# A three-layer transformer forward pass on one core: SBUF addresses of the moving operands shifted against those of the weights

## Chip, core and metric

The program runs on one core of a Trainium2 chip. The metric is device time in microseconds (us), median of the runs shown. TensorE (PE) does the matrix products, VectorE (DVE) and ScalarE (ACT) the elementwise work, GpSimd (POOL) a little of it, and SyncE's queue (SP) issues nearly all loads. "Product" below means one matmul instruction, which multiplies a 128x128 stationary operand (the weights, loaded by an instruction of its own, PEld) with a moving operand of 128 partitions and 128 to 512 columns.

## What is computed

One block with modulation from a vector `c` (pooling, forgetting attention and a gated recurrence side by side, then a gated feed-forward with a causal convolution), a norm, and then two layers of a second kind (three sorts of attention, then a feed-forward with squared ReLU). 256 tokens, 2048 features, float32 throughout. Cut to the products, which hold the work:

```python
mod = silu(c) @ w_ada + b_ada
h = rmsnorm(x, g_mix) * (1 + sc1) + sh1
x = x + gt1 * (mixer(h @ w_in) @ w_out)
h = rmsnorm(x, g_ffn) * (1 + sc2) + sh2
x = x + gt2 * ((silu(conv(h @ w_gate)) * (h @ w_up)) @ w_down)   # 5632 hidden
x = rmsnorm(x, final_g)
for l in range(2):
    x = x + attention(rmsnorm(x) @ w_in_2[l]) @ w_o_2[l]
    x = x + relu(rmsnorm(x) @ w_up_2[l]) ** 2 @ w_down_2[l]       # 8192 hidden
out = rmsnorm(x, norm_final_2)
```

## The kernel before

Activations lie with the features on the partitions: `x`, and its two parts `xh` and `xl` (high and low, both float32r, together called X below), are tiles of 16 row tiles x 256 tokens, 1024 bytes to a row tile and partition. A float32 product is done as three float32r products: high weights by high activations (line 332), high by low (333), low by high (334); `mm_b` on these lines makes nearly all of the work. The weights come from DRAM in pieces of 512 KB (`Unit`): SP loads one to a `raw` tile (seven buffers), ACT rounds it to `whi` (line 136), DVE subtracts to `wlo` (line 137; three buffers each), and PE uses them in 24 products with the 256 tokens as moving operand. In a few places `mm_a` (lines 347 to 349) has it the other way round: slices of `xh` and `xl` are the weights, and `whi` or `wlo`, 256 or 512 columns, is the moving operand.

The order is written out by hand: a list of units is walked in order, splits run up to three units ahead, and small jobs (softmax, norms, convolutions) are generators that advance one stage after each unit. Nothing reorders the instructions afterwards.

The moving operands of `mm_b` are these tiles: X for the projections into a block; `xn` for the pooled and the recurrent part in `w_out`; `uh` and `ul` for `w_ffn_down`; `u0` and `u1` (named `u` in the profile) for `w_down_2`; `mb` for a quarter of `w_o_2`; each with `whi` or `wlo` as the weights.

Tiles are laid in SBUF in the order in which the pools ask for them. The pool `cp`, open for the whole program, has `params`, `ident`, some small tiles, then (lines 490 to 502) `mod` (96 floats to a partition), `cact` (16), `gsc`, `fgg`, `x`, `xh`, `xl` and the rest. The pool `st` behind it holds `raw`, `whi` and `wlo`. On top of both lies the pool of the phase, opened and closed as the program goes: `ffnp` for the first feed-forward has `uh` and `ul` at its foot (line 1138), `mlp0` and `mlp1` for the others have `u0` and `u1` there (line 1801). In the built program each row of `whi` and `wlo` that a product uses as weights starts at a byte address of 192 modulo 512 in its partition. The rows of the moving operands start at: X 160, `uh`, `ul`, `u0` and `u1` 192, `xn` 480, `mb` 0. A row tile being 1024 bytes, every row of a tile has the same residue. As distances from the weights, modulo 512: X 480, `uh`/`ul`/`u` 0, `xn` 288, `mb` 320. In `mm_a`, where `whi` and `wlo` (192) move over X (160), the distance is 32.

Of the kernel before, what the change touches and what calls it, by code (L numbers as in the profile page):

```python
# [17 lines left out]
P = 128  # L18
# [39 lines left out]
def shape_constants():  # L58
    """Arrays that follow from the shapes alone."""
    half = np.arange(P) // 64  # L60
    block = (half[:, None] == half[None, :]).astype(np.float32)
    q = np.arange(S)
    causal = np.where(q[None, :] <= q[:, None], 0.0, NEG).astype(np.float32)
    causal = causal.reshape(2, P, S).transpose(1, 0, 2).reshape(P, 2 * S)
    c = np.arange(64)
    cs = np.clip(c - 8, 0, 48)
    near = np.where((c[None, :] >= cs[:, None]) & (c[None, :] < cs[:, None] + 16), 0.0, NEG)
    near = np.tile(near, (2, 1)).astype(np.float32)
    freqs = np.float32(10000.0) ** (-np.arange(0, 32, 2, dtype=np.float32) / np.float32(32))
    p = np.arange(P) % 64  # L70
    pos = np.where((p // 32 == 0)[:, None], (q // 64)[None, :], (q % 64)[None, :]).astype(np.float32)
    ang = (pos * freqs[p % 16][:, None]).astype(np.float32).astype(np.float64)
    cos = np.cos(ang).astype(np.float32)
    sin = (np.sin(ang) * np.where(p % 32 < 16, -1.0, 1.0)[:, None]).astype(np.float32)
    rec = np.stack([1.0 / np.minimum(np.arange(1, 17), w) for w in WINDOWS]).astype(np.float32)
    rec = np.broadcast_to(rec.reshape(1, 64), (P, 64))
    tri = (np.arange(P)[:, None] <= np.arange(P)[None, :]).astype(np.float32)
    rel = np.arange(-255, 256)
    n = np.abs(rel)
    nf = np.maximum(n, 1).astype(np.float32)  # L80
    large = 8 + (np.log(nf / np.float32(8)) / np.float32(np.log(16.0)) * np.float32(8)).astype(np.int32)
    bucket = np.where(rel > 0, 16, 0) + np.where(n < 8, n, np.minimum(large, 15))
    bucket = np.where(n > 128, 32, bucket)
    onehot = np.zeros((33, 511), np.float32)
    onehot[bucket, np.arange(511)] = 1.0
    return {
        "ident": np.eye(P, dtype=np.float32),
        "mixc": np.ascontiguousarray(np.concatenate([causal, rec, tri], axis=1)),
        "blkc": np.ascontiguousarray(np.concatenate([block, cos, sin, near], axis=1)),
        "onehot": onehot,  # L90
    }
# [27 lines left out]
class Unit:  # L119
    """A [128, nk, ncols] piece of a weight: loaded, cut into two float32r parts, used on the tensor engine."""  # L120
# [24 lines left out]
class Ada:  # L145
    """128 rows x 1024 columns of w_ada times silu(c), summed over the row tiles on the vector engine."""
# [44 lines left out]
def weave(a, b):  # L191
    """the two lists, evenly interleaved"""
# [7 lines left out]
class Builder:  # L200
# [41 lines left out]
    def take(self, tag, shape, dt=F32):  # L242
        """waits (in stages) for a free buffer of the phase pool; returns (number, tile)"""
        while not self.slots[tag]:
            yield
        i = self.slots[tag].popleft()
        return i, self.ph.tile(shape, dt, tag=f"{tag}{i}", name=tag)
# [4 lines left out]
    def bank(self):  # L252
        """the same for a PSUM bank"""
# [23 lines left out]
    def more_groups(self):  # L277
        """two of the banks go over to the column groups"""
# [3 lines left out]
    def fewer_groups(self):  # L282
        """the column groups leave them again; put back once what is in them has been read"""
# [37 lines left out]
    def mm_b(self, u, ps, X, first, last, k0=None, ncols=None):  # L321
        """PSUM[nb] += W[:, nb].T X for the rows of one unit; X = (hi, lo), features on the partitions."""
# [13 lines left out]
    def mm_a(self, u, outs, X, first, last, c0, n, shared=False):  # L336
        """outs[half] += X[:, half].T W for the rows of one unit: tokens on the partitions."""
# [13 lines left out]
    def split_to(self, hi, lo, src, scale=1.0):  # L351
        """hi + lo = src * scale, both float32r."""
# [13 lines left out]
    def units(self, w, kts, c0, ncols, use):  # L366
        """kts: (first row tile, number of row tiles) of each unit"""
        return [Unit(self, w, k, n, c0, ncols, use, i) for i, (k, n) in enumerate(kts)]

    def group(self, w, c0, ncols, kts, X, evac, k0=None, state=None, part="all"):  # L370
        """Units of one column group whose sum stays in PSUM; evac(banks) is a generator started at its end."""
# [17 lines left out]
    def sumsq_add(self, acc, src, first, scale=1.0):  # L389
        """acc (+)= (src * scale)^2"""  # L390
# [8 lines left out]
    def tok_sums(self, ps, *tiles):  # L399
        """Sum over the partitions of tiles of [128, n x 256] -> PSUM [128 tokens, 2]."""  # L400
# [9 lines left out]
    def rstd_of(self, r, ss, n):  # L410
        """r = (ss / n + eps) ** -0.5 of [128, 2]"""
# [9 lines left out]
    def bcast(self, ps, r, dg):  # L421
        """r [128 tokens, 2] -> PSUM [128, 256], each token's value in all partitions."""
# [4 lines left out]
    def rms_now(self, squares, out):  # L427
        """out [128, 256] = 1 / rms of x by token, from tiles of squares"""
# [6 lines left out]
    def rms(self, acc, flag):  # L435
        """the same in stages, to rtok and rbc"""
# [40 lines left out]
    def run(self):  # L477
        tc, nc, io = self.tc, self.nc, self.io
        with ExitStack() as es:
# [10 lines left out]
            self.mod = cp.tile([P, 96], F32, name="mod")  # L490
            self.cact = cp.tile([P, 16], F32, name="cact")
# [4 lines left out]
            self.xl = cp.tile([P, KT, S], F32R, name="xl")  # L496
            self.X = (self.xh, self.xl)
# [31 lines left out]
    def ada_end(self, acc, srcs, then, wait):  # L529
        """the sums over the partitions, to mod; then what needs them"""  # L530
# [20 lines left out]
    def prep(self, q, src, g, sh0, sc0, flag, need=None):  # L551
        """X = src * g * (1 + scale) + shift for four row tiles"""
# [17 lines left out]
    def need(self, flag):  # L570
        """X, once the row tiles of the unit are prepared"""
# [7 lines left out]
    # ================= block 1: mixer =================  # L579
# [6 lines left out]
    def log1p_exp(self, out, e, w):  # L586
        """out = log(1 + e) for 0 <= e <= 1, by the odd series in e / (2 + e); w: three tiles to work in"""
# [15 lines left out]
    def mixer(self):  # L603
# [27 lines left out]
        # silu(c)  # L631
# [7 lines left out]
        # x with features on the partitions, and x / rms(x)  # L639
# [8 lines left out]
        def turn(k):  # L648
            """two row tiles of x and of x / rms(x), the latter by products with a diagonal matrix"""
# [20 lines left out]
        def consts():  # L670
# [5 lines left out]
            # cl = -4 softplus(-lambda), 4 softplus(-lambda)  # L676
# [11 lines left out]
            # halves of the gate biases  # L688
# [16 lines left out]
        # the last two groups of a quarter of the rows stay in PSUM and are the first of the next one  # L705
# [3 lines left out]
        def add_z(name, q, pv, keep):  # L709
            """z (+)= the two banks"""  # L710
# [42 lines left out]
        def forget():  # L753
            """F = cumsum(log sigmoid(f + b)): fq with the tokens on the partitions, fs by head in the first rows of a tile"""
# [100 lines left out]
        # w_out: rows of the recurrent and the pooled part first, the attention rows after  # L855
# [52 lines left out]
    def recurrent(self):  # L908
# [21 lines left out]
        # gelu(y): 0.5 y (1 + tanh(sqrt(2/pi) (y + 0.044715 y^3))), the 0.5 with the product below  # L930
# [19 lines left out]
        # ti = (1 + ti) * xc  (twice the gated input)  # L950
# [13 lines left out]
        # -expm1(2 log_a) = th (1 + a^2), th = tanh(-log_a); its root as v * v^-0.5  # L964
# [19 lines left out]
        # 0.5 of the gate and 0.5 of the gelu  # L984
# [57 lines left out]
    def softmax(self, b, sc, pr, bias, sink, free=None):  # L1042
        """pr = softmax(sc + bias), by rows, with the logit sink beside; frees the bank b"""
# [33 lines left out]
    def fox(self, h):  # L1077
        """One head of the forgetting attention; logits + F[q] - F[k] under the causal mask"""
# [46 lines left out]
    # ================= block 1: gated feed-forward =================  # L1125
# [3 lines left out]
    def ffn(self):  # L1129
# [4 lines left out]
        def start():  # L1134
            self.open_pool("ffnp")
            self.slots["sg"] = deque(range(2))
            ph = self.ph
            F["uh"] = ph.tile([P, KT, S], F32R, name="uh")
# [11 lines left out]
        def gate(j0, g):  # L1150
            """sg = silu(conv(g)) of hidden row tiles j0 .. j0 + 3"""
# [18 lines left out]
        def up(j0, slot, ps):  # L1170
            """rows slot .. slot + 3 of the hidden layer: gate times the two banks in ps"""
# [37 lines left out]
        def acc_units(g, q):  # L1209
            """rows of quarter q for column group g (even: gate, odd: up) of the first 2048 hidden columns"""  # L1210
# [18 lines left out]
        def pair(j0, slot0):  # L1229
            """gate and up of four hidden row tiles"""  # L1230
# [54 lines left out]
        def end():  # L1285
            # x2 = x r1 final_g; its own rstd r2 goes to the next products together with r1
# [47 lines left out]
    def lead(self):  # L1334
        """puts the loads of w_ada, one for one, before the weights of the first block, LEAD ahead"""
# [11 lines left out]
    # ================= block 2 =================  # L1347
    def bias_tables(self):
        """The position biases, spread to [head, query, key] in DRAM."""
# [51 lines left out]
    def layer(self, l):  # L1401
# [4 lines left out]
        def start():  # L1406
# [18 lines left out]
            # row tiles 0-3: A, 4-7: B, 8-15: C; queries, then the heads' outputs  # L1425
# [20 lines left out]
        def kk(dst, c, raw):  # L1446
            """dst[:, 0, c] / [:, 1, c]: high / low part of one head's keys, in both halves of the partitions"""
# [4 lines left out]
        def queries(qs, raw):  # L1452
            """two heads' queries: [high; low] and [low; high]"""
# [5 lines left out]
        def rope(t, gain, done):  # L1459
            """norm per head and rotary embedding of two row tiles, in place"""  # L1460
# [98 lines left out]
        def head(h, keys, v, table, sink, near, kpair, need, values, last):  # L1559
            """one head; queries and output in row tile h // 2"""  # L1560
# [75 lines left out]
        def norm(name, t0, n, dst, d0, gain, after):  # L1636
            """the heads' outputs, normalised over all heads of the kind"""
# [30 lines left out]
        def v_units(name, c0, n, kts, done):  # L1668
            """the values of n heads, tokens on the partitions"""
# [53 lines left out]
        def mb():  # L1723
            # in the place of the outputs of A and the first half of C, which are in X by then
# [73 lines left out]
        def mid():  # L1798
            self.close_pool()
            self.open_pool(f"mlp{l}")  # L1800
            L["u"] = [self.ph.tile([P, KT, S], F32R, name=f"u{i}") for i in range(2)]
# [134 lines left out]
```

## Time and profile before

| | us |
|---|---|
| median of 3 runs | 3420.06 (3419.43 to 3421.57) |
| span of the profiled execution, first to last instruction | 3419.7 |
| PE busy in it | 3282.7 (96%) |
| DVE busy | 2213.9 (65%) |
| ACT busy | 1629.8 (48%) |
| POOL busy | 294.4 (9%) |
| DMA | 684 MB, mean 200 GB/s |

The profiled execution ended within 0.4 us of the median, so its span can be used for it. A matmul's record is some 283 ns long, but several are under way at a time, so the time between the starts of two products that follow each other, and not the record's length, tells what one costs PE. That time is got from a stretch in which PE doesn't pause: the records that touch the stretch, divided into its length plus one record. In a view of one tile alone, it is the busy time less one record, divided by the count less one.

### The profile page before, as it was taken

Reading aid. Unit: us, or ns where it says so; the run is one execution under the profiler, and the core shown is the slowest. Engines: PE = TensorE matmul, PEld = TensorE weight load, DVE = VectorE, ACT = ScalarE, POOL = GpSimd, SP = SyncE. Lnnn points to the kernel's source line nnn. Section 1 sums busy time; section 2 is a strip of 40 time slices with the busy share of each in tenths; the row PEclk is TensorE's granted clock in tenths of the full one; section 3 lists DMA queues with packets and bytes.
Section 4 is the critical chain, followed back from the end, with each engine's and each line's share of the span. In section 5 each row is a group of like instructions: output and inputs, shape, how many; then the busy total and the mean of one; then the engine's idle time right before and its main releaser. Section 6 shows DMA issues by size and latency. Waiting matters only on the chain.

```text
span 3419.7 us, 64015 instructions
## 1 busy us (share of the span) xinstructions
PE 3282.7 (96%) x26612; PEld 3231.9 (95%) x26612; DVE 2213.9 (65%) x2921; ACT 1629.8 (48%) x2236; POOL 294.4 (9%) x250
## 2 busy tenths in 40 slices
PE   7989899979999998999999999999999999999998
PEld 7988889979999998989999999998889999999998
DVE  7898887537745668976545454556897655545454
ACT  4436345424434456865434343445775533334344
POOL 0021100000000032111000000012110100000000
PEclk9999999999999999999999999999999999999999
DMA  9986896659866554545666665665454656666563
GB/s 360 336 286 224 300 318 225 187 169 304 273 200 187 184 160 122 162 143 180 185 185 185 185 186 183 186 182 154 133 161 153 182 184 185 185 185 185 183 186 125
DMA packets 390722, 683.96 MB, mean 200 GB/s; under 512 B 40823, under 2 KB 97952, under 8 KB 390176
## 3 DMA queue, kind: packets, MB, share of 16 engines
q1 hardware_dynamic: 390144, 679.56, 62.8%
q8 instruction: 208, 3.41, 0.4%
q14 instruction: 82, 0.67, 0.1%
q10 hardware_dynamic: 288, 0.31, 0.0%
HBM read 677.62 MB, written 8.46 MB: 201 GB/s over the span
## 4 chain that ended last, share of the span: by engine, by line
PE 77%; DVE 6%; DMA 2%; issue 2%; ACT 2%; SPq 1%; POOL 0%; ACTq 0%; DVEq 0%; POOLq 0%
PE pg L334 24%; PE pg L332 24%; PE pg L333 24%; DVE wlo L137 2%; ACT whi L136 1%; DMA raw<-in_w_ffn_up 1%; DMA raw<-in_w_ffn_gate 1%; DMA raw<-in_w_out 1%; PE pa L1620 1%; PE pa L1073 1%; DVE qs L1457 1%; DVE kB L362 0%; PE pa L1556 0%; DVE pr L1049 0%; DVE ada L171 0%
## 5 line engine op out<-in xcount | busy, mean ns | idle before, releaser
L137 DVE TENSOR_TENSOR wlo<-raw,whi 128x1024 fp32r<-128x1024 f32 x1064 | 1319.0, 1241 | 1089.0 <-ACT whi L136 1084.9
L136 ACT ACTIVATE whi<-raw 128x1024 fp32r<-128x1024 f32 x1064 | 1123.4, 1058 | 1554.0 <-PE pg L333 1254.1
L332 PE MATMUL pg<-xh,whi 128*128 128x256 f32 x5184 | 1478.6, 285 | 24.6 <-ACT whi L136 20.0
L334 PE MATMUL pg<-xh,wlo 128*128 128x256 f32 x5184 | 1468.2, 283 | 16.3 <-DVE wlo L137 16.2
L333 PE MATMUL pg<-xl,whi 128*128 128x256 f32 x5184 | 1467.0, 283 | 1.8 <-DVE xl L565 1.1
L332 PEld LDWEIGHTS pg<-xh,whi 128*128 128x128 f32 x5184 | 988.3, 191 | 30.4 <-ACT whi L136 21.2
L334 PEld LDWEIGHTS pg<-xh,wlo 128*128 128x128 f32 x5184 | 987.0, 190 | 20.8 <-DVE wlo L137 20.4
L333 PEld LDWEIGHTS pg<-xl,whi 128*128 128x128 f32 x5184 | 987.7, 191 | 6.9 <-issue 2.7
L332 PE MATMUL pg<-u,whi 128*128 128x256 f32 x2048 | 579.9, 283 | 0.0
L333 PE MATMUL pg<-u,whi 128*128 128x256 f32 x2048 | 579.5, 283 | 0.0
L334 PE MATMUL pg<-u,wlo 128*128 128x256 f32 x2048 | 579.5, 283 | 0.0
L333 PEld LDWEIGHTS pg<-u,whi 128*128 128x128 f32 x2048 | 393.1, 192 | 0.0
L334 PEld LDWEIGHTS pg<-u,wlo 128*128 128x128 f32 x2048 | 393.1, 192 | 0.0
L332 PEld LDWEIGHTS pg<-u,whi 128*128 128x128 f32 x2048 | 393.1, 192 | 0.0
L171 DVE SCALAR_TENSOR_TENSOR ada<-raw,cact,ada 128x1024 f32<-128x1024 f32 x180 | 234.8, 1304 | 19.1 <-DMA raw<-in_w_ada 18.1
L397 POOL TENSOR_TENSOR acc<-acc,t 128x512 f32<-128x512 f32 (+1 forms) x73 | 97.1, 1345 | 1372.3 <-ACT t L396 1361.0
L334 PE MATMUL pg<-uh,wlo 128*128 128x256 f32 x704 | 199.3, 283 | 0.0
L332 PE MATMUL pg<-uh,whi 128*128 128x256 f32 x704 | 199.3, 283 | 0.0
L333 PE MATMUL pg<-ul,whi 128*128 128x256 f32 x704 | 199.2, 283 | 0.0
L1820 POOL TENSOR_TENSOR y<-y 128x1024 f32<-128x1024 f32 x32 | 61.6, 1927 | 1200.0 <-ACT u L1819 1200.0
L332 PEld LDWEIGHTS pg<-uh,whi 128*128 128x128 f32 x704 | 135.1, 192 | 0.9 <-issue 0.9
L334 PEld LDWEIGHTS pg<-uh,wlo 128*128 128x128 f32 x704 | 135.1, 192 | 0.2 <-DVE wlo L137 0.2
(323 smaller groups left out, 2815.8 us busy)
## 6 DMA issues: line engine op xcount, KB each, us to landing
raw<-in_w_up SPq DMA_DIRECT2D x256, 512.0 KB
raw<-in_w_down SPq DMA_DIRECT2D x256, 512.0 KB
raw<-in_w_ada SPq DMA_DIRECT2D x192, 512.0 KB
raw<-in_w_in SPq DMA_DIRECT2D x192, 512.0 KB
raw<-in_w_ffn_gate SPq DMA_DIRECT2D x88, 512.0 KB
raw<-in_w_ffn_up SPq DMA_DIRECT2D x88, 512.0 KB
raw<-in_w_ffn_down SPq DMA_DIRECT2D x88, 512.0 KB
raw<-in_w_o SPq DMA_DIRECT2D x64, 512.0 KB
```

Of the source, the lines that this page charges most:

```text
L136: b.nc.scalar.activation(hi[:, :n], self.raw[:, :n], AF.Copy)
L137: b.nc.vector.tensor_tensor(lo[:, :n], self.raw[:, :n], hi[:, :n].bitcast(F32), ALU.subtract)
L171: b.nc.vector.scalar_tensor_tensor(g["acc"], self.raw, cs, g["acc"], ALU.mult, ALU.add)
L332: mm(o, wh, xh[:, k0 + j, :], start=st, stop=False, skip_group_check=True)
L333: mm(o, wh, xl[:, k0 + j, :], start=False, stop=False, skip_group_check=True)
L334: mm(o, wl, xh[:, k0 + j, :], start=False, stop=last and j == u.nk - 1, skip_group_check=True)
L397: nc.gpsimd.tensor_tensor(acc, acc, t, ALU.add)
L1073: self.nc.tensor.transpose(ps[:, k * S + i * P : k * S + (i + 1) * P], pr[:, i, k * P : (k + 1) * P], self.ident)
L1457: nc.vector.tensor_tensor(qs[b, h, :], raw[a], qs[a, h, :].bitcast(F32), ALU.subtract)
L1620: nc.tensor.matmul(o, v()[:, k].rearrange("p a d -> p (a d)"), pt[1][:, c, k, :], start=n == 0, stop=n == 3)
L1820: nc.gpsimd.tensor_tensor(flat(y), flat(y), flat(y), ALU.mult)
```

## The change

Three places change where tiles lie; the docstrings and comments that it also takes out have no effect.

- `mod` and `cact` (384 and 64 bytes to a partition) are allocated behind `xl` instead of ahead of `gsc`. `gsc`, `fgg`, `x`, `xh` and `xl` lie 448 bytes lower; everything behind them stays where it was.
- The pool `ffnp` gets an unused tile of 160 bytes at its foot, so that `uh`, `ul` and what lies above them move up by 160.
- The pools `mlp0` and `mlp1` get one of 288 bytes, so that `u0`, `u1` and what lies above them move up by 288.

```diff
-            self.mod = cp.tile([P, 96], F32, name="mod")
-            self.cact = cp.tile([P, 16], F32, name="cact")
             self.gsc = cp.tile([P, 16], F32, name="gsc")
             self.fgg = cp.tile([P, 16], F32, name="fgg")
             self.x = cp.tile([P, KT, S], F32, name="x")
             self.xh = cp.tile([P, KT, S], F32R, name="xh")
             self.xl = cp.tile([P, KT, S], F32R, name="xl")
+            self.mod = cp.tile([P, 96], F32, name="mod")
+            self.cact = cp.tile([P, 16], F32, name="cact")
...
             self.open_pool("ffnp")
             self.slots["sg"] = deque(range(2))
             ph = self.ph
+
+            ph.tile([P, 40], F32, name="skew")
             F["uh"] = ph.tile([P, KT, S], F32R, name="uh")
             F["ul"] = ph.tile([P, KT, S], F32R, name="ul")
...
             self.open_pool(f"mlp{l}")
+            self.ph.tile([P, 72], F32, name="skew")
             L["u"] = [self.ph.tile([P, KT, S], F32R, name=f"u{i}") for i in range(2)]
```

The distances from the weights, modulo 512, are then: X 32, `uh` and `ul` 160, `u0` and `u1` 288; `xn` and `mb` stay at 288 and 320, and in `mm_a` the distance becomes 480. On every engine the built program has the same instructions in the same order with the same waits as before; only addresses differ.

## Rows read from the trace of the kernel before

**Rows 1.** The page: busy time of PE; shares of the chain that ended last.

```profile
PE 3282.7 (96%) x26612; PEld 3231.9 (95%) x26612; DVE 2213.9 (65%) x2921; ACT 1629.8 (48%) x2236; POOL 294.4 (9%) x250
...
PE 77%; DVE 6%; DMA 2%; issue 2%; ACT 2%; SPq 1%; POOL 0%; ACTq 0%; DVEq 0%; POOLq 0%
```

**Rows 2.** Groups of PE's instructions by line and shape: count, busy, mean ns, idle before.

```profile
L332 PE MATMUL pg<-xh,whi 128*128 128x256 f32 x5184 | 1478.6, 285 | 24.6 <-ACT whi L136 20.0 <-ACT xh L562 3.0 <-DVE zp L719 0.9
...
L332 PE MATMUL pg<-u,whi 128*128 128x256 f32 x2048 | 579.9, 283 | 0.0
...
L332 PE MATMUL pg<-uh,whi 128*128 128x256 f32 x704 | 199.3, 283 | 0.0
...
L347 PE MATMUL pg<-whi,xh 128*128 128x512 f32 x128 | 54.3, 424 | 7.3 <-DVE zq L721 7.1 <-ACT whi L136 0.3
...
L347 PE MATMUL pg<-whi,xh 128*128 128x256 f32 x64 | 19.5, 304 | 0.0
```

**Rows 3.** Busy time in stretches (us; engine busy, xinstructions; PEclk): tile `u` alone.

```profile
1676.00:1770.00 94.00, 92.31 (x768) 92.22 (x768) 1.37 (x2) 1.04 (x1) 1.00 0.60 184
```

**Rows 4.** The same for tile `uh` alone (two of each three products).

```profile
928.00:1021.00 93.00, 92.31 (x512) 79.92 (x512) 1.37 (x2) 1.04 (x1) 1.00 0.66 197
```

**Rows 5.** The same, all instructions, in a stretch of X alone.

```profile
1022.00:1152.00 130.00, 130.00 (x1101) 130.00 (x1100) 71.06 (x78) 58.91 (x63) 0.00 (x0) 1.00 0.60 188
```

**Rows 6.** The same for tile `xn` alone.

```profile
346.00:366.50 20.50, 19.99 (x170) 19.91 (x170) 0.00 (x0) 0.00 (x0) 0.00 (x0) 1.00 0.92 311
```

**Rows 7.** The same for tile `mb` alone.

```profile
1562.00:1586.00 24.00, 22.78 (x192) 22.68 (x192) 0.00 (x0) 0.00 (x0) 1.00 0.59 178
```

**Rows 8.** Timeline of PE (start us, us): first and last of 71 products of `mm_a`.

```profile
2359.70 0.28 PE L348 MATMUL pg<-wlo,xh 128*128 128x256 f32 x1
...
2367.87 0.28 PE L349 MATMUL pg<-whi,xl 128*128 128x256 f32 x1
```

**Rows 9.** Line 758, weights of 8 columns: shortest, median, longest ns; first, last start.

```profile
L758 PE MATMUL pa<-xh,wfh x16: 276/276/281, 207.1 to 212.2; 128*8 128x256 f32 x16
```

**Rows 10.** All engines by stage: us, PE, PEld, DVE, ACT, POOL, PEclk, DMA share, GB/s.

```profile
0.00:540.00 540.00, 484.99 (x3625) 462.23 (x3626) 456.51 (x570) 254.38 (x364) 63.31 (x83) 0.96 0.88 305
540.00:720.00 180.00, 179.17 (x1493) 177.73 (x1492) 110.03 (x129) 87.56 (x98) 0.00 (x0) 1.00 0.58 180
720.00:780.00 60.00, 41.47 (x295) 39.78 (x293) 24.43 (x26) 15.63 (x17) 0.00 (x0) 0.83 0.57 190
780.00:1232.00 452.00, 451.78 (x3796) 451.38 (x3797) 280.53 (x307) 205.71 (x233) 16.81 (x22) 1.00 0.71 224
1232.00:1512.00 280.00, 251.88 (x1890) 239.80 (x1889) 237.49 (x521) 194.85 (x410) 54.96 (x44) 0.96 0.47 142
1512.00:2340.00 828.00, 828.00 (x6953) 827.73 (x6952) 449.40 (x454) 345.00 (x362) 56.82 (x34) 1.00 0.60 183
2584.00:3400.00 816.00, 816.00 (x6855) 815.73 (x6854) 438.78 (x446) 345.73 (x372) 53.50 (x32) 1.00 0.59 179
```

**Rows 11.** The same stages, tile `xl` alone: PE, PEld, DVE, PEclk, DMA share, GB/s.

```profile
0.00:540.00 540.00, 275.38 (x935) 179.25 (x935) 16.53 (x40) 0.96 0.88 305
540.00:720.00 180.00, 67.46 (x241) 45.24 (x241) 0.00 (x0) 1.00 0.58 180
...
780.00:1232.00 452.00, 226.44 (x806) 151.97 (x807) 5.22 (x12) 1.00 0.71 224
1232.00:1512.00 280.00, 144.37 (x491) 95.52 (x491) 5.14 (x9) 0.96 0.47 142
1512.00:2340.00 828.00, 341.29 (x1216) 228.96 (x1215) 16.08 (x33) 1.00 0.60 183
2340.00:2584.00 244.00, 123.55 (x419) 81.55 (x419) 2.72 (x4) 0.96 0.47 142
2584.00:3420.00 836.00, 334.06 (x1189) 223.97 (x1189) 10.11 (x18) 0.99 0.58 177
```

## The prediction, made before the changed kernel ran

> **What bounds the kernel now.** I read the page first, for which engine fills the span: PE is busy 96% of it and makes 77% of the chain that ended last [rows 1]. Then the view by line: three lines of `mm_b` hold nearly all of PE's work, 5184 triples of products with X, 2048 with `u`, 704 with `uh` [rows 2], that is 15,552, 6144 and 2112 products. Then the stages: from 540 to 720 us, 780 to 1232, 1512 to 2340 and 2584 to 3400 PE hardly pauses (179.2 of 180 us, 451.8 of 452, 828 of 828, 816 of 816), at the full granted clock (1.00), with DVE at 54 to 62% busy and the DMA engines at 58 to 71% [rows 10]. In the first 540 us, between 720 and 780, and in the two attention stages PE pauses and others come last; there DMA (0.88 and 305 GB/s in the first 540 us) or DVE (237 of 280 us in the first attention) is close to full [rows 10].
>
> So in some 2280 us of 3420 the time is the count of products by the interval from the start of one to the next. That interval is what the change can move, and the trace has it for five distances between moving operand and weights. All are 256 columns on 128x128 weights at a granted clock of 1.00:
> - distance 0, `u`: (92.31 - 0.28) / 767 = 120.0 ns [rows 3]; `uh`/`ul`: 768 products in the same busy time (the 512 shown are the `uh` ones), again 120.0 ns [rows 4].
> - distance 480, X: (130 + 0.28) / 1101 = 118.3 ns [rows 5].
> - distance 320, `mb`: (22.78 - 0.28) / 191 = 117.8 ns [rows 7].
> - distance 288, `xn`: (19.99 - 0.28) / 169 = 116.6 ns [rows 6].
> - distance 32, `mm_a`: 8.17 us / 70 = 116.7 ns [rows 8].
>
> `u`, `uh`, `xn`, `mb` and X stand on the same three lines, with the same shape, type and clock; what differs is the tile, that is its address. A product on the same X tiles but with weights of 8 columns takes (212.2 - 207.1) / 45 = 113.3 ns [rows 9], so about 3 to 7 ns of each interval come with the load of the 128 weight columns that runs beside it. I read this as two streams of PE out of SBUF, moving operand and next weights, that get in each other's way by their relative address, most at distance 0. The moving operand's own address can't be it: `u` and the `whi` of `mm_a` both start at 192 modulo 512, and take 120.0 and 116.7 ns.
>
> [...]
>
> **The change part by part.** No instruction, order or wait is altered, so each part is a count of products by a difference of intervals.
>
> `u`, 0 to 288: after the change its rows stand at 480 modulo 512 and the weights at 192, just as those of `xn` do now. 6144 products, all in stages where PE never pauses: 6144 x (120.0 - 116.7) = 20.3 us. I take 116.7 for `xn` and `mm_a` alike; the 0.1 between them is the views' rounding.
>
> X, 480 to 32: 32 is shown by `mm_a`, with the roles of the tiles exchanged, and 288, which differs from 32 by 256, gives the same 116.7 in `mm_b`. So 118.3 to 116.7, which is 1.63 ns before rounding. One product in three with X reads `xl`, so the counts of `xl` by stage tell where X is used: 241 + 806 + 1216 + 1189 = 3452 from 540 to 720, 780 to 1232, 1512 to 2340 and after 2584 [rows 11], 10,356 products, in stages bound by PE: 16.9 us. The other stages: in the first 540 us 935, less 64 of `mm_a`, is 2613 products, 4.3 us; but DMA fills most of it, and a faster PE waits for the next load, so I count a quarter, 1.1 us. In the two attention stages 491 + 419, less 128 of `mm_a`, is 2346 products, 3.8 us; DVE is busy 85% of the first and PE 90%, and I count half, 1.9 us. The 99 or so triples between 720 and 780, where PE is busy 41.5 of 60 us [rows 10], count nothing.
>
> `uh`/`ul`, 0 to 160: no row has 160. Bounds: not above distance 0, 120.0 (no gain); not below the product with small weights, 113.3 (14.2 us). If distances that differ by 256 act alike, as 32 and 288 do, 160 lies between 64 (that is 320, 117.8) and 224 (that is 480, 118.3), and further from 0 than either. I take 117.5, halfway from the best interval with full weights, 116.7, to the interval of X: 2112 x 2.5 = 5.3 us.
>
> `mm_a`, 32 to 480: here the change goes the wrong way. 192 products of 256 columns and 384 of 512 [rows 2]. At X's present interval the first lose 1.63 ns each, 0.3 us; the others, having two 256s of columns, at most 3.3 ns, 1.3 us. They lie in the first 540 us and in the attention stages, so half: 0.8 us lost.
>
> Everything else keeps its distance: `xn`, `mb`, the attention's own products. Elementwise work gets other addresses too, but DVE and ACT have free time in the stages that PE bounds.
>
> Who would be late next in these stages? A unit of 24 products takes 2.88 us at 120.0 and 2.80 at 116.7, and wants 512 KB, which is 187 GB/s at the faster pace, against 183 now; between 780 and 1232 the loads run at 224 on average with PE full [rows 10]. DVE goes from 54% to 56%. Neither comes near.
>
> Sum: 20.3 + 16.9 + 1.1 + 1.9 + 5.3 - 0.8 = 44.7 us. From the span 3419.7 that is 3375.0; from the median 3420.06 it is 3375.4 us.
>
> **Rivals.**
> - X gains nothing: 32 is good with the roles as in `mm_a` but not with `whi` as the weights, and X stays at 118.3. Then 19.9 us fall away: 3395.3. For it: no row has distance 32 in `mm_b`. Against it: 288 in `mm_b`, and equal intervals at 32 and 288.
> - The freed time comes back as waits for DVE or loads in the PE-bound stages. If half of it did, 3397.7. Against it: the idle shares above; and between 1512 and 2340 us and between 2584 and 3400 PE waits for nobody at all.
> [...]
> - Slower: at 32 the moving rows follow so close behind the weights that they collide more than at 480. Place: X in the PE-bound stages; price, at 123 ns (as far above `u` as `u` is above 117): 10,356 x 4.7 = 48.7 us lost against 20.3 + 5.3 gained, some 3443. It decides from 118.3 + 25.6 / 10.356 = 120.8 ns on, more than any of the five distances shows.
>
> **How the numbers follow.** Forecast 0.82, X without gain 0.08, half eaten by waits 0.04, no effect 0.03, slower 0.03. The range of the forecast: if all of X's gain in the mixed stages counts (5.1 more), `uh` comes to 113.3 (9 more, unlikely at the same time) and `mm_a` costs nothing (0.8), the time is 3360.5; if the mixed stages give nothing (3.0), `uh` stays at 120.0 (5.3) and `mm_a` costs all (0.8), 3384.5. A few pauses more or less in the mixed stages, where the granted clock is 0.83 to 0.96 [rows 10] and so falls to its lower level now and then, can move it by some us on either side. I give 3362 to 3388; it leaves out all four rivals, 0.18. A measurement of this kernel can tell 0.2%, 6.8 us, from no change: faster by more than that are the forecast and the first two rivals, 0.94; within it 0.03; slower 0.03.
>
> **What would show it.** In the changed kernel's stretches: `u` at 116.7 ns a product, X at 116.7, `uh` between 116.7 and 118.3, `xn` and `mb` as now at 116.6 and 117.8, `mm_a` at 118.3; PE still full from 1512 us (or where that stage then begins) to the next attention; shorter stages after 780 us by about 1.4% for X and 2.8% for `u`. What would make it wrong: an interval for X above 118, which the exchange of roles could hide from me; new waits of PE for `whi` or `wlo` in the stages that have none; or the first 540 us changing by more than 2 us.

## The result, and the profile after

The changed kernel takes 3382.68 us (median of 4 runs, 3375.75 to 3386.76) against 3420.18 before (4 runs by now): 37.5 us less, a ratio of 0.989 (95% interval 0.9875 to 0.9903). Forecast were 3375.4 us and 44.7 us less, with a range of 3362 to 3388. The profiled execution has a span of 3381.7 us, 38.0 less than the one of before; a second set of four runs of the same kernel gave 3381.69 (3379.57 to 3383.47).

The page after: busy time by engine, and the chain that ended last.

```profile
PE 3238.2 (96%) x26612; PEld 3186.4 (94%) x26612; DVE 2213.5 (65%) x2921; ACT 1630.8 (48%) x2236; POOL 294.7 (9%) x250
...
PE 75%; DVE 7%; issue 2%; ACT 2%; DMA 2%; POOL 0%; SPq 0%; ACTq 0%; DVEq 0%; POOLq 0%
```

PE is busy 44.5 us less with the same number of instructions, DVE and ACT as long as in [rows 1]. The same products are started closer together. PE's idle time grew from 137.0 to 143.5 us: of the 44.5 us 6.5 came back as pauses. In the two long stages that PE bounds it stays full:

```profile
1508.00:2319.00 811.00, 811.00 (x6946) 810.71 (x6945) 448.95 (x454) 344.64 (x361) 56.85 (x34) 1.00 0.64 187
2581.00:3361.00 780.00, 779.94 (x6685) 779.48 (x6685) 420.96 (x417) 333.62 (x350) 53.75 (x32) 1.00 0.62 183
```

Busy time of stretches by tile shows it (us; PE, PEld and so on, each busy time with its count; granted clock, DMA share, GB/s): first `u`, which answers to [rows 3], then `uh` as in [rows 4].

```profile
1670.00:1762.00 92.00, 89.76 (x768) 89.67 (x768) 1.37 (x2) 1.05 (x1) 1.00 0.62 189
```

```profile
924.00:1018.00 94.00, 91.30 (x512) 78.76 (x512) 1.37 (x2) 1.05 (x1) 1.00 0.69 199
```

`u` went from 120.0 to (89.76 - 0.28) / 767 = 116.7 ns, `uh` here to (91.30 - 0.28) / 767 = 118.7. All instructions in stretches of one tile alone: X as in [rows 5], X in three other places, and last `uh` in another place.

```profile
1017.00:1147.00 130.00, 130.00 (x1116) 130.00 (x1116) 72.17 (x80) 60.02 (x64) 0.00 (x0) 1.00 0.65 190
831.00:920.00 89.00, 89.00 (x758) 89.00 (x757) 66.76 (x70) 40.44 (x43) 0.00 (x0) 1.00 0.90 287
564.70:620.00 55.30, 55.30 (x471) 55.30 (x471) 42.80 (x57) 30.70 (x37) 0.00 (x0) 1.00 0.63 191
1762.00:1842.00 80.00, 80.00 (x688) 80.00 (x687) 42.78 (x41) 32.70 (x32) 5.75 (x3) 1.00 0.65 190
640.00:714.00 74.00, 74.00 (x633) 74.00 (x632) 33.09 (x28) 31.18 (x34) 0.00 (x0) 1.00 0.60 183
```

X stands at 130.28 / 1116 = 116.7 ns in the first, at 89.28 / 758 = 117.8 in the second, at 55.58 / 471 = 118.0 in the third (117.8 from start to start), at 80.28 / 688 = 116.7 in the fourth; `uh` at 74.28 / 633 = 117.3. One count more or less is 0.1 to 0.3 ns here. So X has two intervals at one and the same distance, and so has `uh`. The same two views for `mb`, whose distance the change leaves at 320, in the first layer and in the second:

```profile
1556.00:1581.00 25.00, 22.78 (x192) 22.69 (x192) 0.00 (x0) 0.00 (x0) 1.00 0.63 187
```

```profile
2624.00:2649.00 25.00, 21.93 (x192) 21.84 (x192) 0.00 (x0) 0.00 (x0) 1.00 0.64 188
```

The first is as in [rows 7], 117.8 ns; the second is 113.4, at the same distance, with the same instructions and clock. And `mm_a`, whose distance went from 32 to 480, first and last of 71 products on PE's timeline (start us, duration us), as in [rows 8]:

```profile
2339.11 0.28 PE L348 MATMUL pg<-wlo,xh 128*128 128x256 f32 x1
...
2347.40 0.28 PE L349 MATMUL pg<-whi,xl 128*128 128x256 f32 x1
```

8.29 us / 70 = 118.4 ns, where it was 116.7. That is X's old interval at X's old distance, with the roles exchanged. The products of `mm_a` with 512 columns went through the same exchange; first and last of 48 in a row, before and after:

```profile
69.66 0.39 PE L347 MATMUL pg<-whi,xh 128*128 128x512 f32 x1
...
80.61 0.39 PE L349 MATMUL pg<-whi,xl 128*128 128x512 f32 x1
```

```profile
69.35 0.40 PE L347 MATMUL pg<-whi,xh 128*128 128x512 f32 x1
...
80.31 0.40 PE L349 MATMUL pg<-whi,xl 128*128 128x512 f32 x1
```

10.95 / 47 = 233.0 ns at 32 and 10.96 / 47 = 233.2 at 480, at a granted clock of 1.00: the products of 512 columns show no effect of this distance.

### The profile page after: what moved, and what is told of

The parts are those of the page before. It is cut to its first block, busy times and chain, and to the rows that moved or that the text cites. A ratio compares the mean times of both kernels' runs of the same rounds, so it can differ in the third digit from the quotient of the medians.

```text
span 3381.7 us, 64015 instructions
## 1 busy us (share of the span) xinstructions
PE 3238.2 (96%) x26612; PEld 3186.4 (94%) x26612; DVE 2213.5 (65%) x2921; ACT 1630.8 (48%) x2236; POOL 294.7 (9%) x250
## 4 chain that ended last, share of the span: by engine, by line
PE 75%; DVE 7%; issue 2%; ACT 2%; DMA 2%; POOL 0%; SPq 0%; ACTq 0%; DVEq 0%; POOLq 0%
PE pg L334 24%; PE pg L332 24%; PE pg L333 24%; DVE wlo L137 3%; ACT whi L136 1%; DMA raw<-in_w_ffn_up 1%; DMA raw<-in_w_ada 1%; DVE ada L171 1%; DVE qs L1459 1%; PE pa L1622 1%; PE pa L1073 1%; DVE kB L362 0%; PE pa L1558 0%; DVE pr L1049 0%; DVE y L1489 0%
## 5 line engine op out<-in xcount | busy, mean ns | idle before, releaser
L332 PE MATMUL pg<-u,whi 128*128 128x256 f32 x2048 | 572.1, 279 | 0.0
L333 PE MATMUL pg<-u,whi 128*128 128x256 f32 x2048 | 571.7, 279 | 0.0
L334 PE MATMUL pg<-u,wlo 128*128 128x256 f32 x2048 | 571.6, 279 | 0.0
L333 PEld LDWEIGHTS pg<-u,whi 128*128 128x128 f32 x2048 | 384.9, 188 | 0.0
L334 PEld LDWEIGHTS pg<-u,wlo 128*128 128x128 f32 x2048 | 384.9, 188 | 0.0
L332 PEld LDWEIGHTS pg<-u,whi 128*128 128x128 f32 x2048 | 384.9, 188 | 0.0
```

The lines of the kernel that those rows point to most:

```text
L332: mm(o, wh, xh[:, k0 + j, :], start=st, stop=False, skip_group_check=True)
L333: mm(o, wh, xl[:, k0 + j, :], start=False, stop=False, skip_group_check=True)
L334: mm(o, wl, xh[:, k0 + j, :], start=False, stop=last and j == u.nk - 1, skip_group_check=True)
```

## The experiments

All are edits of the kernel before, and the profiles are of one execution each. "Interval" is the time from the start of one product of 256 columns to the next, in a stretch in which PE doesn't pause; "distance" is always moving operand from weights, modulo 512.

**One edit at a time.** `x_only` has the first edit alone, `u_only` the third.

> The first of the three edits alone: X moves from distance 480 to 32, u and uh stay at 0. Theory A (the distance between moving operand and weights sets the interval): X at 116.7 ns in most stretches, at 117.8 in some, as in the changed kernel; u and uh at 120.0. Stretches of X shorter by 1.28 us per 768 products; in all 12 to 16 us less than before, about 3405. Theory B (the interval belongs to the tile or to its own address, not to the distance): X could go anywhere; u and uh as before too.

> The third edit alone: u moves from distance 0 to 288, X stays at 480, uh at 0. Theory A: u at 116.7 ns, 2.54 us less per 768 products, 20.3 us in all, about 3400; X at 118.3 and uh at 120.0 as before; no new pauses. A spread between runs that is as small as before's 2 us would say that the 11 us spread of the changed kernel comes with X or uh at their new distances; a spread of 10 us would say that it comes with u.

`x_only`: 3410.87 us (3404.87 to 3414.2), ratio 0.997 (0.996 to 0.998), 10.5 us less. `u_only`: 3400.83 us (3397.8 to 3402.02), ratio 0.9939 (0.9925 to 0.9952), 20.6 us less. In `x_only`, X in the first block's feed-forward behind `uh`, X between two stretches of `u`, X in the first block's feed-forward ahead of `uh`, and `u` alone:

```profile
1018.00:1148.00 130.00, 130.00 (x1107) 130.00 (x1106) 71.29 (x78) 59.30 (x64) 0.00 (x0) 1.00 0.65 189
1766.00:1846.00 80.00, 80.00 (x681) 80.00 (x681) 42.37 (x41) 32.80 (x32) 5.76 (x3) 1.00 0.64 187
...
565.00:620.00 55.00, 55.00 (x473) 55.00 (x473) 43.13 (x61) 30.15 (x36) 0.00 (x0) 1.00 0.63 191
```

```profile
1672.00:1766.00 94.00, 92.32 (x768) 92.22 (x768) 1.37 (x2) 1.04 (x1) 1.00 0.62 183
```

`u` is at 120.0, as expected. X is at 117.7 and 117.9 behind `uh` and `u`, and at 55.28 / 473 = 116.9 before them: with the same addresses as in the changed kernel, where the first two stood at 116.7 and the third, the other way round, at 117.8. The 12 to 16 us expected were missed for the same reason: more of X than thought ran at 117.8. In `u_only`, X and then `u`:

```profile
1768.50:1848.50 80.00, 80.00 (x678) 80.00 (x677) 42.03 (x41) 33.02 (x32) 5.77 (x3) 1.00 0.64 185
```

```profile
1677.00:1769.00 92.00, 89.77 (x768) 89.68 (x768) 1.37 (x2) 1.04 (x1) 1.00 0.63 189
```

`u` is at 116.7 and X at 118.4 as before. The term of `u` held: 8 stretches' worth of 2.54 us, 20.3, in the trace, and 20.6 by the times. The edit of X was worth less alone than beside the others: 10.5 + 20.6 = 31.1, against 37.5 and, in the second set, 40.6 for all three. By the trace `uh` has 4.2 us of the difference by its own intervals (its edit alone was not run); 2.2 and 5.3 us are left. The six stretches of X that lie behind `u` would account for 6 x 768 products x 1.11 ns = 5.1 us, which X gets only where `u` is at 288 too. The intervals of the times are too wide to tell more.

**Moving the weights in place of X.**

```diff
+            cp.tile([P, 112], F32, name="skew")
             nc.scalar.dma_start(self.params, io["params"])
```

> X stays where it was in the kernel before; 448 unused bytes ahead of raw, whi and wlo move the weights and all that lies above them, so that the distance is 32 for X, 0 for u and uh, 288 for xn, 320 for mb. Theory A: X at 116.7 ns (117.8 in some stretches) though none of its own addresses changed; u and uh at 120.0 though theirs did. Theory B: X at 118.3 as before; u, whose own address is now 128 modulo 512, at another interval than 120.0.

One run, 3411.05 us, the time of `x_only`. X at the three places of `x_only`, then `u`:

```profile
565.00:620.00 55.00, 55.00 (x474) 55.00 (x473) 43.13 (x58) 30.06 (x37) 0.00 (x0) 1.00 0.64 192
1020.00:1150.00 130.00, 130.00 (x1107) 130.00 (x1106) 71.30 (x78) 59.30 (x64) 0.00 (x0) 1.00 0.64 188
1767.00:1847.00 80.00, 80.00 (x682) 80.00 (x681) 42.46 (x41) 32.71 (x32) 5.76 (x3) 1.00 0.64 187
```

```profile
1673.00:1767.00 94.00, 92.32 (x768) 92.22 (x768) 1.37 (x2) 1.04 (x1) 1.00 0.62 184
```

X has the intervals of `x_only` stretch by stretch, 116.6, 117.7 and 117.7, though X didn't move; `u` is at 120.0 at another address of its own, its distance still 0. So it is the distance and not the tile's own address: theory B falls.

**Other distances.** `scan_a` has four of them:

```diff
-            self.zero = cp.tile([P, 1], F32, name="zero")
-            self.mod = cp.tile([P, 96], F32, name="mod")
...
             self.xl = cp.tile([P, KT, S], F32R, name="xl")
+            self.mod = cp.tile([P, 96], F32, name="mod")
+            self.zero = cp.tile([P, 1], F32, name="zero")
...
             ph = self.ph
+            self.ph.tile([P, 32], F32, name="skew")
...
             self.open_pool(f"mlp{l}")
+            self.ph.tile([P, (24, 48)[l]], F32, name="skew")
```

> Four new distances in one look: X 64, uh 128, u of the first layer 96, u of the second 192. Theory A with a period of 256: X at 64 as mb at 320, that is 117.8 or 113.3 ns, the two values that mb showed in the changed kernel; uh at 128, and u at 96 and 192, each at one or two values of their own between 113 and 119. If the period is 128 instead: uh at 128 at 120.0 as at 0, u at 96 at 118.3 as X at 480 (224), u at 192 as at 64.

3404.61 us. X at 64 in a long stretch and in a short one; then `uh` at 128, `u` at 96 and `u` at 192:

```profile
1764.00:1844.00 80.00, 80.00 (x681) 80.00 (x680) 42.51 (x41) 33.41 (x32) 5.76 (x3) 1.00 0.64 185
```

```profile
564.30:580.00 15.70, 15.70 (x141) 15.70 (x140) 12.47 (x18) 8.20 (x11) 0.00 (x0) 1.00 0.64 188
```

```profile
924.50:1017.50 93.00, 91.30 (x512) 78.67 (x512) 1.37 (x2) 1.04 (x1) 1.00 0.69 200
```

```profile
1670.50:1764.50 94.00, 92.32 (x768) 92.22 (x768) 1.37 (x2) 1.04 (x1) 1.00 0.62 184
```

```profile
2753.50:2845.00 91.50, 90.61 (x768) 90.53 (x768) 1.37 (x2) 1.04 (x1) 1.00 0.63 187
```

X is at 117.9, in the short stretch at 15.98 / 141 = 113.3, the two values of `mb`; 128 gives 118.7, 96 gives 120.0, as slow as distance 0 and above the 119 expected at most, and 192 gives 117.8. A period of 128 would have 96 at the 118.3 of 224 and 128 at the 120.0 of 0; neither is so. A period of 256 agrees with the pairs that were seen: 32 with 288, 64 with 320, and 192 with 448, which `mm_a` has here (8.25 us / 70 = 117.8). For the other distances it is carried over and not shown.

`scan_b` puts X at 32 as the changed kernel does, and `u` and `uh` at distances that a slice of a wider tile gives:

```diff
-            L["u"] = [self.ph.tile([P, KT, S], F32R, name=f"u{i}") for i in range(2)]
+            off = ((4, 4), (12, 12))[l]
+            big = [self.ph.tile([P, KT * S + 128], F32R, name=f"u{i}") for i in range(2)]
+            L["u"] = [t[:, a : a + KT * S].rearrange("p (k n) -> p k n", k=KT) for t, a in zip(big, off)]
```

> Distances that are no multiple of 32: u of the first layer 16, u of the second 48, uh 80; X stays at 32. If what collides are lines of 32 bytes: 16 at an interval between those of 0 and 32, 120.0 to 116.7; 48 between 116.7 and 117.8; 80 between 117.8 and 120.0 (96). If the chip sees only the line's number: 16 as 0 (120.0) and 48 as 32 (116.7), 80 as 64.

3388.18 us. `u` at 16, `u` at 48, `uh` at 80:

```profile
1666.50:1757.50 91.00, 89.77 (x768) 89.67 (x768) 1.37 (x2) 1.04 (x1) 1.00 0.64 188
```

```profile
2735.50:2828.50 93.00, 91.04 (x768) 90.94 (x768) 1.37 (x2) 1.05 (x1) 1.00 0.62 186
```

```profile
924.00:1015.50 91.50, 91.04 (x512) 78.58 (x512) 1.37 (x2) 1.05 (x1) 1.00 0.70 200
```

16 gives 116.7, as good as 32; 48 and 80 give 118.3. Neither expectation held. That the line's number alone counts is out, since 16 isn't at the 120.0 of 0. Nor does the interval run evenly between multiples of 32: 80 lies between its neighbours, 48 above both of its own.

`scan_c` gives the high and the low part distances of their own (offsets 32 and 160, 64 and 192 bytes in `u`, 32 and 64 in `uh`, in the same way as `scan_b`); `scan_d` moves `wlo` alone by 32 bytes, so that the third product of a triple differs:

```diff
+        if not hasattr(b, "skw"):
+            b.skw = b.st.tile([P, 8], F32, name="skw")
         lo = b.st.tile([P, 1024], F32R, tag="wlo", name="wlo", bufs=HB)
```

> High and low part at distances of their own: u of the first layer 32 and 160, of the second 64 and 192, uh 32 and ul 64; X stays at 32. If each product's interval follows from its own distance to the weights beside it, the mean of a triple is two thirds of the high part's interval and one third of the low part's: 117.3, 117.8 and 117.0. If the products of a triple hand a state on to each other, it can be something else, down to 113.3.

> wlo lies 32 bytes further on than before, whi doesn't, so that the third product of each triple (line 334) has a distance of its own: X and uh 32 and 0, u of the first layer 64 and 32, u of the second 192 and 160. If only the distance of a product to the weights that are loaded beside it counted, the products with line 334's distance would be a third: X at (2 x 116.7 + 120.0) / 3 = 117.8. If the interval depends on the whole triple, anything from 113.3 to 120.0.

`scan_c`, 3386.29 us: `u` of the first layer, then two stretches of `u` of the second.

```profile
1666.00:1759.50 93.50, 91.19 (x768) 91.08 (x768) 1.37 (x2) 1.05 (x1) 1.00 0.62 186
```

```profile
2738.50:2830.00 91.50, 90.62 (x768) 90.52 (x768) 1.37 (x2) 1.04 (x1) 1.00 0.64 187
```

```profile
2918.00:3010.00 92.00, 90.05 (x768) 89.96 (x768) 1.37 (x2) 1.04 (x1) 1.00 0.64 188
```

118.5, then 117.8 and 117.0, where the expected means over the triple's distances were 117.3 and 117.8: the stretch from 2739 us has the mean, the two behind it don't. The `uh` part, 117.0 expected, came to 117.8. With 117.8 for 32 and 118.7 for 160 the first mean would be 118.1, still below 118.5. `scan_d`, 3403.56 us: X at 32 and 0 between two stretches of `u` at 64 and 32, and between two at 192 and 160.

```profile
1763.00:1853.00 90.00, 90.00 (x759) 90.00 (x758) 46.71 (x46) 36.77 (x35) 5.75 (x3) 1.00 0.61 184
...
2844.00:2931.00 87.00, 87.00 (x745) 87.00 (x745) 45.38 (x44) 35.74 (x34) 5.76 (x3) 1.00 0.62 187
```

90.28 / 759 = 118.9 and 87.28 / 745 = 117.2 for the same X; the mean of a triple would be 117.8, and X behind `uh` (from 1018 us) has it. So in these runs a product's interval doesn't follow from its own distance alone: what ran before it counts too (118.9 and 117.2 here). That the rest of the triple counts was not shown by itself.

**One common distance.** `all32` is the changed kernel with `uh` at 288 (72 floats in place of 40); `all64` has X, `uh` and `u` at 64 (X as in `scan_a`, 16 floats of padding in both pools).

> The changed kernel with uh and ul at 288 instead of 160, so that X, uh and u all stand at 32 modulo 256. Theory A with a memory (a stretch without a pause hands its interval on to the next tile at the same distance modulo 256): uh at 116.7 ns where it follows an X at 116.7, at 117.8 otherwise, 2 to 4 us less in uh than the changed kernel, and X no slower; about 3379. Rival (each stretch draws its interval anew): the stretches of u and X in the second feed-forwards would show 116.7 and 117.8 mixed, as they didn't in the changed kernel, and the time would be the changed kernel's or up to 10 us more.

> X, uh and u all at 64, where 113.3 and 117.8 ns have been seen. Memory: once a stretch without a pause has 113.3, all that follow keep it until PE next pauses; the stages without a pause could lose 800 us x 4.5 / 117.8 = 30 us each against 117.8. If 113.3 is never entered, all stretches at 117.8 and about 3392. Rival (the interval follows from the distance alone): all at 117.8.

`all32` took 3378.39 us (3378.01 to 3379.56), ratio 0.9878 (0.9861 to 0.9894). It ran a second time beside the changed kernel:

> The changed kernel once more, beside the next one on the same chip. Median about 3383, spread some 10 us, since X in the first block's feed-forward is now at 116.7 and now at 117.8 ns and uh at 117.3 or 118.7.

> X at 32, uh and u at 288 once more. If handing on a common interval is what makes it faster, it stays 3 to 6 us below the changed kernel, about 3378, with uh and X between 780 and 1232 us at one common interval per stretch without a pause.

The changed kernel: 3381.69 us, 0.9881 (0.9864 to 0.9897). `all32`: 3379.06 us (3374.52 to 3384.9), 0.9876 (0.9861 to 0.9891). It is 3 to 4 us lower both times, but the intervals overlap: by the times alone it isn't shown to be faster. X, `uh` and X in succession, in the first and in the second profile of `all32`:

```profile
832.60:921.00 88.40, 88.40 (x761) 88.40 (x760) 66.96 (x72) 40.36 (x43) 0.00 (x0) 1.00 0.90 288
927.00:1015.00 88.00, 88.00 (x757) 88.00 (x756) 43.99 (x41) 34.51 (x33) 0.00 (x0) 1.00 0.71 202
1017.00:1147.00 130.00, 130.00 (x1116) 130.00 (x1116) 72.22 (x80) 59.61 (x64) 0.00 (x0) 1.00 0.66 190
```

```profile
832.00:920.00 88.00, 88.00 (x750) 88.00 (x748) 66.10 (x70) 40.43 (x43) 0.00 (x0) 1.00 0.88 287
927.00:1015.00 88.00, 88.00 (x750) 88.00 (x749) 43.24 (x40) 34.01 (x33) 0.00 (x0) 1.00 0.67 199
1017.00:1147.00 130.00, 130.00 (x1106) 130.00 (x1106) 71.67 (x79) 59.33 (x64) 0.00 (x0) 1.00 0.61 189
```

In the first all three stand at 116.5 to 116.7, in the second at 117.7 to 117.8, and it stays so over some 370 us: same kernel, same addresses, another value taken at the start and handed on from tile to tile. The values are those of distance 32; which one is taken isn't decided by the layout. `all64`, 3395.34 us, shows 113.2 in a short stretch (16.08 / 142, from 564 us on; 113.3 from start to start) and 117.8 in the long ones:

```profile
563.60:579.40 15.80, 15.80 (x142) 15.80 (x141) 12.66 (x18) 8.31 (x11) 0.00 (x0) 1.00 0.65 191
1671.00:1759.00 88.00, 88.00 (x749) 88.00 (x749) 43.48 (x40) 33.57 (x32) 1.92 (x1) 1.00 0.64 187
```

113.3 was entered at the same place in `scan_a` and lost at PE's next pause, at 580 us, in both. How to enter it elsewhere stays open; an estimate from the counts in [rows 2], 24,000 products at 113.3 instead of 116.7, is some 80 us.

## Why the prediction was right, and where it was off

- **What bounds the kernel**: right. PE is full in the same stages. Its pauses there (time between two starts beyond 0.145 us, less one interval) came to 7.3 us where they had been 6.2, and the rest of what was spared there is in the interval.
- **`u`**: 20.3 us forecast, 20.1 by the trace (each stretch of 768 products is 2.55 us shorter; 191 products near the end ran at 117.8), 20.6 by the times of `u_only`. That `xn` stood at the very residues that `u` was to get made this the safest term.
- **X in the PE-bound stages**: 16.9 forecast, about 15.2 found, which is what these stages became shorter by, less `u` and `uh`. It includes 0.9 for `mb`, which wasn't expected to move, so X alone gave some 14.3. The direction was right, and the size of the interval, 116.7, in most stretches; but 1479 of the X products there ran at 117.8, which costs 1.6 us, and the pauses took some 1.2. The gain of `mb` hid part of this by luck. That a distance has one interval is the step that failed: the trace of before had only one steady value for X, `u` and `mb` each, and I took this for a rule.
- **`uh`**: 5.3 forecast, 4.2 found. 160, of which no row told, has 117.3 and 118.7; 1005 of the 2110 products ran at 118.7, above the 116.7 to 118.3 that the prediction gave as its sign. That 117.5 lies between the two is luck: it was the middle of two intervals at other distances.
- **`mm_a`**: 0.8 lost was forecast. The interval of 118.4 at 256 columns is what the exchange of roles said; but most of the term was for 512 columns, and these didn't move, 233.0 and 233.2, so at most 192 x 1.63 ns = 0.3 us was lost. That the distance decides at 256 columns, and not tile or role, is borne out by `weights_moved` for the tile (X at 116.6 to 117.7 at its old address) and by `mm_a` for the role (118.4 at 480, where X had 118.3).
- **What the weights cost**: the prediction put 3 to 7 ns of each interval down to loading 128 columns of weights, since 113.3 was seen with 8 columns alone. That step isn't borne out: with 128 columns `mb` at 320 and X at 64 ran at 113.3 to 113.4 too. As a lower bound 113.3 held.
- **The stages in which PE pauses**: 3.0 gained was forecast, and 0.8 of it given back by `mm_a`. Measured between the same products, the first 540 us became 0.3 us shorter, the loads' pause from 720 to 784 us 0.5 longer, the first attention (1240 to 1512 before) 2.6 longer and the second 1.2 shorter: 1.5 us lost instead of 2.2 gained. The first attention took 271.8 us before, and in the profiles of the other kernels 270.9 to 274.4, with X at 32 in both the shortest and the longest; so X's distance doesn't settle it, and why it differs from run to run stays open. Counting a quarter and a half of the gain there was too much.
- **Sum**: the terms fall short by 0.2 (`u`), 1.7 (X), 1.1 (`uh`) and 3.7 (mixed stages and `mm_a`), which is the 6.7 us between 44.7 and the 38.0 of the profiles.
- **The rivals**: X gained, so the first is out. The half eaten by waits is out: 6.5 of 44.5 us came back as pauses, most of them in the mixed stages. No effect, 0.03, is out: the time fell by 37.5 us, `u` went from 120.0 to 116.7 ns, and in `weights_moved` X went from 118.3 to between 116.6 and 117.7 though its own addresses stayed. Slower is out for 32, where X stood at 116.7 and 117.8; of the distances seen, 0 and 96, where `u` stood at 120.0, are the slowest.
- The spread of 2 us that the kernel before showed at first came from 3 runs: in the later sets its runs lie between 3416.6 and 3424.6, and no wider spread of the changed kernel can be claimed.

## What to carry to other kernels

Where PE runs products back to back, take the interval between starts from the count in a stretch without a pause, tile by tile: differences of a few nanoseconds between tiles of the same shape (256 columns), on the same line, at the same clock (116.6 to 120.0 ns before) went here with how the moving operand lay against the weights, and a pad of 288 bytes at a pool's foot took `u` from 120.0 to 116.7 without touching any instruction. Put tiles that follow each other without a pause at one good distance (32 modulo 256 here; 16 did as well in one kernel), since a stretch handed its interval on in some of these runs: X behind `u` stood at 116.7 in the changed kernel, and at 117.7 and 117.9 in `weights_moved` and `x_only`, where `u` was at 0. That doing so for `uh` too (`all32`) makes the program faster is not shown. Look for a place in the old trace that already has the new layout: it gave the terms that held best.

## What the runs showed of the hardware

Intervals by distance modulo 256, 256 columns on 128x128 float32r weights at a granted clock of 1.00, as seen here (those with one star in one kernel alone):

| distance | ns |
|---|---|
| 0 | 120.0 |
| 16 * | 116.7 |
| 32 (also as 288) | 116.7 or 117.8 (120.0 in some stretches of 96) |
| 48 * | 118.3 |
| 64 (also as 320) | 117.8 or 113.3 |
| 80 * | 118.3 (120.0 in stretches of 96 and 141) |
| 96 * | 120.0 |
| 128 * | 118.7 |
| 160 * | 117.3 or 118.7 (120.0 over 434 products in the second profile of the changed kernel) |
| 192 (also as 448) | 117.8 (113.4 over the last 71 products of `u` in `scan_a`) |
| 224 (seen as 480 alone) | 118.3 |

Products of 512 columns took 233.0 and 233.2 ns at 32 and at 480.

Not expected: that several distances have more than one steady interval (the table's numbers are means over a stretch); and that the one taken held across a change of tile where both stood at 32 modulo 256: X and `u` of the changed kernel ran at 116.7 from 1601 to 2309 us, while X behind `u` at 0 ran at 117.7 (`weights_moved`) and 117.9 (`x_only`). Where it was lost, PE had not always paused: in the changed kernel X went from 116.7 to 117.8 at 2309 us behind eight products of another line and shape (404, one column), and in `all32` X went from 116.7 to 117.8 at 473 us, where a single product started 124 ns after the one before it. Nor does the layout fix the value: `mb` of the first attention layer ran at 113.4 in the first profile of `all32` and at 117.8 in the second, and behind `u` at 48 (`scan_b`) X at 32 took 117.8, 116.7 and 117.8. That two reads collide is the prediction's reading and was not shown; the runs show that the distance between the two operands counts (`u` at 120.0 at 0 and at 116.7 at 288, with the same instructions). What happens between the two streams, and what fixes the value at a start, no run here tells.
